# A hybrid layer's kernel: keys laid out by residue, the sample's values in loads of four rows, and an order of five engines computed in the source

## The chip, the core and the metric

One core of a Trainium2 chip runs the whole kernel. The metric is the device time of one execution in microseconds (us). A core has a matrix engine (TensorE; PE in the profile, its weight loads PEld), a vector engine (VectorE, DVE), a scalar engine (ScalarE, ACT), a general engine (GpSimd, POOL) and a sync engine (SyncE, SP). They read and write two on-chip memories, SBUF and PSUM (where matmuls put their sums), of 128 partitions each, and each runs its own list of instructions in order; semaphores hold an instruction back until what it needs is done. All transfers of this kernel (DMAs, transposing ones too) are issued by SP, from one list.

## The reference

One step of a hybrid decoder layer for a prompt of 2048 tokens and a sample of 8 sequences with 8 tokens each. Mixer A is attention over three dilated windows, mixer B a gated linear attention (GLA):

```
h = rmsnorm(x, norm_w);  z = h @ w_in
q, k, v, qb, kb, vb, g_lr, gate_a, gate_b = split(z)
q = rope(rmsnorm(q), pos);  k = rope(rmsnorm(k), pos)        # 8 heads of 64
# for (window, dil) in (128,1), (512,4), (2048,16):
#   softmax over the keys at distance 0, dil, 2*dil, ... window
o_a = sum over the branches of softmax(lse)[branch] * o[branch]
o_b = rmsnorm(gla(qb, kb, vb, log_sigmoid(g_lr @ w_gate_up + b_gate) / 16, s0))
y = x + concat(o_a * silu(gate_a), o_b * silu(gate_b)) @ w_out
```

For the sample the keys and values of the past come from caches of 2048 rows for each sequence (`cache_k_win`, `cache_v_win`). Beside `y` the new keys, values and GLA states are returned.

## The kernel before

The prompt is cut into 16 tiles of 128 tokens. A projection of a tile is a chain of f16 matmuls over 8 blocks of the model's width, in three products of high and low halves (L1120); the normed and rotated queries and keys go to DRAM as f16 (`qp_d`, `kp_d`) and come back transposed by DMA, so that the head's dimension lies along the partitions.

The program is written in the order of its stages. `first(m)` projects v, q and k of the four tiles of block m (m = 0 to 3). For each block and each half of the heads (`pp` = 0, 1) follow the units of attention: `unit(m, pp, 1, x)` is branch 1 (128 consecutive queries against that block of keys and the one before), `unit(m, pp, 2, x)` is branch 2 (the queries of the 512-row block with residue x modulo 4, against the same residue of this block and the one before). `branch3(r)` does residue r modulo 16 over the whole prompt. A unit's pieces go through `attend`: scores on PE (L408), mask and row maximum on DVE (L416), the exponential on ACT (L419), transposes of the probabilities on PE (L426), their copies to SBUF on DVE, ACT or POOL (L389 to L393), the product with v on PE (L441), and the sum of the two halves on DVE (L458).

The block's keys lie in `kk`, a tile [128, 8 heads, 2 slots, 512]: a slot holds one block of 512 keys in their own order, and blocks alternate between the slots. `keys(m, a)` (L841) fills it by a transposing DMA of 128 consecutive rows. `queries(m, pp)` (L853) does the same for the queries, and `swapped` makes on DVE (L845, L846) a second copy of a query tile with the halves of the partitions exchanged. In a score matmul the queries are the stationary operand (PEld) and the keys the moving one. So branch 1 moves runs of consecutive keys, and branch 2 every fourth key, `k[:, :, x::4]`: 256 keys, or 128 in block 0, which has no block before it. Branch 3 loads its own `T_q` and `T_k` (L936, L938) by transposing DMAs of every sixteenth row and swaps the queries with the same two DVE copies.

Woven into these stages are the later projections (qkb, g, vb, gb) and, for the sample's keys, products on POOL with a reduction on DVE (`pr` L980, `sck` L981). Then come the GLA (L120 to L300) and the output stage: the branches are combined, transposed (`tm` L1453, `mt_s` L1465 for the sample) and projected (`Y`, `Y_s` L1488), with the residual added on DVE (L1495). Woven into the output stage is the sample's attention: for each of four pairs of sequences, `sample_pair` loads the cache's values piece by piece (`sv` L1763, 256 KB, one row of the sequence to each partition, eight buffers) and multiplies them on PE with f32 operands (`OS` L1737): 14 steps, one for the new tokens and 13 for pieces of the cache, each step four matmuls that write four column groups of one PSUM tile.

The order is set in three ways: `weave` and the credit of `pump` interleave generators in the source; the tile framework then reorders every engine's list by a simulation of its own; and for a few instructions the source overrules it (`manual_schedule` on ACT around `prep_first`, `issue_after` on two weight loads in `first`).

## Time and profile before

| | us |
|---|---|
| median of 3 runs | 1424.39 |
| lowest and highest run | 1419.62, 1426.09 |
| span of the profiled execution | 1424.9 |
| PE busy in it | 1285.0 |
| DVE busy | 1018.0 |
| ACT busy | 843.7 |
| POOL busy | 621.9 |

The profiled execution's own time is its span, from the first to the last instruction of its one core; what lies around it isn't listed. The page gives each engine's busy time as a share of that span. A view by windows gives the busy time of each engine in a stretch of the span together with the mean clock that the throttle granted to TensorE (PEclk, 1.00 is full speed). The view of waits says what an engine's next instruction waited for, in all, how often, and the longest. A timeline lists runs of the same instruction: start, length, and the count. For `OS` the trace holds two records for each matmul (256 for 128 instructions with `P3x`); all other matmuls quoted here have one.

### The profile page before, as it was taken

Reading aid. Unit: us, or ns where it says so; the run is one execution under the profiler, and the core shown is the slowest. Engines: PE = TensorE matmul, PEld = TensorE weight load, DVE = VectorE, ACT = ScalarE, POOL = GpSimd, SP = SyncE. Lnnn points to the kernel's source line nnn. Section 1 sums busy time; section 2 is a strip of 40 time slices with the busy share of each in tenths; the row PEclk is TensorE's granted clock in tenths of the full one; section 3 lists DMA queues with packets and bytes.
Section 4 is the critical chain, followed back from the end, with each engine's and each line's share of the span. In section 5 each row is a group of like instructions: output and inputs, shape, how many; then the busy total and the mean of one; then the engine's idle time right before and its main releaser. Section 6 shows DMA issues by size and latency. Waiting matters only on the chain.

```text
span 1424.9 us, 26506 instructions
## 1 busy us (share of the span) xinstructions
PE 1285.0 (90%) x8942; PEld 743.6 (52%) x8942; DVE 1018.0 (71%) x2459; ACT 843.7 (59%) x2259; POOL 621.9 (44%) x564
## 2 busy tenths in 40 slices
PE   5989999889898898996889999889999989999997
PEld 2434555455455554664667666666555434444343
DVE  6797697789798967666775357898877797773222
ACT  6466787667377775875677665777876542221120
POOL 0144355566577455554421486556551264340000
PEclk9999999999999899997999999999999999999998
DMA  8469756678966797888976444242235759998661
GB/s 297 156 188 255 192 161 150 182 203 215 240 165 173 208 288 239 260 217 228 234 190 179 149 123 116 87 153 91 88 119 176 267 179 344 359 316 267 221 215 63
DMA packets 246874, 283.27 MB, mean 199 GB/s; under 512 B 117889, under 2 KB 148690, under 8 KB 246738
## 3 DMA queue, kind: packets, MB, share of 16 engines
q1 hardware_dynamic: 246738, 281.57, 67.1%
q8 instruction: 71, 1.16, 0.4%
q14 instruction: 65, 0.53, 0.1%
HBM read 183.19 MB, written 75.24 MB: 181 GB/s over the span
## 4 chain that ended last, share of the span: by engine, by line
PE 35%; DVE 25%; DMA 16%; ACT 11%; issue 7%; POOL 4%; SPq 2%; DVEq 0%; POOLq 0%; ACTq 0%
PE Y L1488 7%; PE acc_g L1120 3%; PE acc_vb L1120 3%; PE acc_k L1120 3%; DMA k<-in_cache_k_win 2%; POOL pr L980 2%; PE s L408 2%; PE OS L1737 2%; PE acc_qkb L1120 2%; ACT p L419 2%; DMA o_d<-o 2%; DMA oc<-o_d 2%; DVE p L416 2%; PE acc_v L1120 2%; DMA T_q<-qp_d 2%
## 5 line engine op out<-in xcount | busy, mean ns | idle before, releaser
L980 POOL TENSOR_TENSOR pr<-k,qb 128x512 f32<-128x512 f32 x128 | 171.8, 1342 | 184.9 <-DVE sck L981 113.9
L1120 PEld LDWEIGHTS <-hr 128*128 128x128 f16 x1824 | 177.7, 100 | 138.2 <-issue 17.6
L419 ACT ACTIVATE p<-p,o 128x256 f32<-128x256 f32 (+1 forms) x384 | 173.1, 453 | 86.0 <-DVE o L416 83.3
L1120 PEld LDWEIGHTS <-hl 128*128 128x128 f16 x1248 | 123.2, 100 | 146.6 <-issue 22.2
L1488 PE MATMUL Y<-w_o,mh 128*128 128x512 f16 x768 | 182.9, 385 | 8.3 <-ACT mh L1454 4.9
L416 DVE CUSTOM_DVE_ANT_0 p<-s,m3w,scl_s 128x256 f32<-128x256 f32 (+1 forms) x384 | 143.6, 419 | 39.0 <-DMA o_d<-o 20.3
L393 POOL TENSOR_TENSOR pt<-p,pt 128x512 f16<-128x512 f32 (+1 forms) x80 | 98.3, 1229 | 139.6 <-ACT pt L392 107.3
L441 PE MATMUL O<-v,pt 128*128 128x128 f16 x1200 | 116.1, 224 | 25.3 <-POOL pt L393 10.0
L426 PE MATMUL t<-ident,p 128*128 128x128 f32 x600 | 119.0, 289 | 14.5 <-ACT p L419 9.2
L1488 PEld LDWEIGHTS <-mh 128*128 128x128 f16 x768 | 72.5, 99 | 103.7 <-issue 25.2
L408 PE MATMUL s<-kk,qq 128*128 128x256 f16 (+1 forms) x512 | 105.7, 326 | 17.5 <-DVE o L416 12.4
L981 DVE TENSOR_REDUCE sck<-pr 128x8 f32<-128x512 f32 x128 | 87.0, 680 | 44.0 <-POOL pr L980 43.7
L441 PEld LDWEIGHTS <-pt 128*128 128x128 f16 x1200 | 86.6, 101 | 54.6 <-POOL pt L393 13.6
L1120 PE MATMUL acc_g<-w_g,hr 128*128 128x272 f16 (+1 forms) x768 | 103.3, 285 | 1.9 <-DVE so_g L677 1.0
L1120 PE MATMUL acc_v<-w_v,hl 128*128 128x512 f16 x384 | 99.5, 405 | 4.6 <-DMA hl<-ht 3.7
L426 PEld LDWEIGHTS t<-ident,p 128*128 128x128 f32 x600 | 73.5, 146 | 43.2 <-ACT p L419 26.4
L1120 PE MATMUL acc_q<-w_q,hl 128*128 128x512 f16 x384 | 92.0, 380 | 1.9 <-ACT zs_q L703 1.4
L1120 PE MATMUL acc_k<-w_k,hl 128*128 128x512 f16 x384 | 91.3, 382 | 2.5 <-ACT w_k L658 1.3
L1454 ACT ACTIVATE mh<-tm 128x1024 f16<-128x1024 f16 x32 | 31.7, 1019 | 104.1 <-PE tm L1453 97.7
L1120 PE MATMUL acc_gb<-w_gb,hr 128*128 128x512 f16 x384 | 90.0, 388 | 2.1 <-DVE so_gb L677 2.1
L1120 PE MATMUL acc_vb<-w_vb,hr 128*128 128x512 f16 x384 | 89.3, 379 | 1.6 <-DVE so_g L677 1.6
L212 ACT ACTIVATE E<-D_e 128x256 f32<-128x256 f32 (+1 forms) x168 | 67.7, 411 | 27.1 <-DVE ks L219 17.6
(533 smaller groups left out, 2628.1 us busy)
## 6 DMA issues: line engine op xcount, KB each, us to landing
k<-in_cache_k_win SPq DMA_DIRECT2D x104, 256.0 KB, 4.3
sv<-in_cache_v_win SPq DMA_DIRECT2D x104, 256.0 KB, 5.4
hr<-h_d SPq DMA_DIRECT2D x44, 512.0 KB, 4.1
qb<-q_d SPq DMA_DIRECT2D x64, 256.0 KB, 4.6
oc<-o_d SPq DMA_DIRECT2D x48, 264.0 KB, 5.8
o_d<-o SPq DMA_DIRECT2D x64, 132.0 KB, 3.9
x<-in_x_prompt SPq DMA_DIRECT2D x16, 512.0 KB, 5.8
h_d<-hl SPq DMA_DIRECT2D x16, 512.0 KB, 4.7
```

The costliest lines, as they stand in the source:

```text
L212: ACT.activation(E[rows, i, :n], D[rows, half], AF.Exp, scale=1.0 / 16.0)
L393: POOL.tensor_tensor(l, f, h, ALU.subtract)
L408: PE.matmul(s_ps[:, i * w : (i + 1) * w], q, k, start=(n == 0), stop=(n == len(prods) - 1),)
L416: DVE.tensor_tensor_reduce(s[:, sl], s_ps[:, sl], mask, neg, BIG, ALU.add, ALU.min, nmf(i))
L419: ACT.activation(s[:, sl], s[:, sl], AF.Exp, bias=nmf(i), scale=-1.0, accum_out=denf(i))
L426: PE.transpose(p_ps[:, i * P : (i + 1) * P], t["s"][:, i * P : (i + 1) * P], ident[:])
L441: PE.matmul(o_, t["pt"][:, c, (i * nb + b) * P : (i * nb + b + 1) * P], vf(i, b), start=(n == 0), stop=(n == 2 * nb - 1),)
L980: POOL.tensor_tensor(pr[:], kt, qt, ALU.mult)
L981: DVE.tensor_reduce(out, pr[:].rearrange("p (u k d) -> p u k d", u=2, k=4), AX.X, ALU.add)
L1120: PE.matmul(z, a_[:, k, :], w[:, p_, k, cols], start=(k == 0 and i == 0), stop=(k == KT - 1 and i == 2),)
L1454: ACT.activation(mhl[:, a], pt[:], AF.Copy)
L1488: PE.matmul(Y[:], a_[:, k, :], w_[:, part, k, :512], start=(i == 0), stop=(i == len(prods) - 1),)
```

## The change

It has three parts.

**Keys by residue.** `kk` becomes [128, 8 heads, 4 residues, 2 slots, 128]. `keys(m, a)` transposes the rows a, a+4, a+8, ... of the 512-row block in place of 128 consecutive rows. Branch 2 then reads its 256 keys (the two slots of one residue) as one consecutive run; branch 1 reads its keys as runs of 32, one for each residue and block of 128. The order of branch 1's keys is thus permuted, and with it the rows of its `v` load and a copy of the mask, `m1w`. The queries stay as they were.

**Values in loads of four rows.** A pair's 26 loads of `sv` become 8: for each of its two sequences one of 256 KB ("w") and three of 1 MB ("b2", "b30", "b34"), each with four neighbouring rows of 2 KB to a partition, in six buffers of 1 MB and two of 256 KB. The weight of the sample's attention in `weave` goes from 64 steps to 36.

**A planner.** At the end of the source `Plan` reads all traced instructions with the tiles they touch, builds their dependencies (`dep`), the order that tiles and buffers force (`behind`), a price for each instruction (`price`), and its longest way to the end of the program (`rank`). `order` is a list scheduler for all five engines at once, which always takes the ready instruction with the longest way to the end, except that on PE it keeps f32 matmuls together (`bias`). `fix` chains each engine's list into a fixed order. `manual_schedule` and `issue_after` are removed. Some constants move between pools, `ident8` is gone.

```
-            r0 = 512 * m + P * a
-            SP.dma_start_transpose(kk[:, :, m % 2, P * a : P * a + P], kp_d[r0 : r0 + P, :])
+            SP.dma_start_transpose(
+                kk[:, :, a, m % 2, :], by4(kp_d[512 * m : 512 * m + 512, :])[a]
+            )
...
-                SP.dma_start(vt[:], sel(vp_d[:, pp * 512 : (pp + 1) * 512]))
+                rows = sel(vp_d[:, pp * 512 : (pp + 1) * 512])
+                SP.dma_start(vt[:], by4(rows) if br == 1 else rows)
...
+                    k = kk[:, 4 * pp + 2 * a + i]
+                    q = [qs_[m, pp][:, order_, 2 * a + i] for order_ in range(2)]
                     if br == 2:
-                        qs = slice(x, 512, 4)
-                        of = lambda k: k[:, :, qs] if nb == 2 else k[:, m % 2, qs]
+                        k = k[:, x] if nb == 2 else k[:, x, m % 2]
+                        q = [f[:, x::4] for f in q]
                     else:
...
+                        k = k.rearrange("p r s (b c) -> p r (s b) c", c=32)
+                        k = k.rearrange("p r b c -> p b r c")[:, of]
...
-        with tc.manual_schedule(engines={mybir.EngineType.Activation}):
-            prep_first(load_w("v"))
+        prep_first(load_w("v"))
...
-                                with tc.issue_after(last_low[0].ins):
-                                    at_once(load_w("q"))
+                                at_once(load_w("q"))
...
+            pieces.append((
+                "b2", [lambda x, c=c: p2[:, x, 32 * c : 32 * c + 32] for c in range(4)],
+                lambda v: v[W - 512 : W, :].rearrange("(j r) c -> j r c", r=4),
+            ))
...
-                    v = ssk.tile([P, 512], F32, name=f"sv_{bp}_{bb}_{i}", tag="sv", bufs=8)
+                    v = ssk.tile(
+                        [P, n, 512], F32, name=f"sv_{bp}_{bb}_{nm_}", tag=f"sv{n}",
+                        bufs=2 if n == 1 else 6,
+                    )
...
-        weave(out, [sample_attention(), 4 * 16])
+        weave(out, [sample_attention(), 4 * 9])
+
+    plan = Plan(tc, nc)
+    far = plan.rank()
+    plan.fix(plan.order([-f for f in far], 2000.0)[1])
```

The parts of the new class that the order rests on:

```
    def price(self):
...
                if ts[0].dtype == F32 and i.is_transpose:
                    busy, late = 109.0 * max(1.0, n / 128), 272.0
                elif ts[0].dtype == F32:
                    busy = max(108.0, 1.69 * n)
                    late = busy + 165
                    self.slow.add(len(self.busy))
                else:
                    n *= 2 if step >= 4 else 1
                    busy, late = max(n / 2.4 + 2.4, 55.5), 165 + n / 2.4
...
            elif e == "SP":
                if kind == "InstDmaTransposeAnt":
                    total = cells(ts[0]) * ts[0].ap[0][1] * 2
                    busy = 1400.0 if total < 500000 else 2800.0
                    late = 18.0 * total / 256 / 16
                    self.lands[len(self.busy)] = 1700.0
...
    def rank(self):
...
            far[n] = max(
                own + max((far[x] for x in self.nxt[n]), default=0.0),
                max((far[x] for x in self.then[n]), default=0.0),
            )
        return far

    def order(self, prio, bias=0.0):
...
            line = now[e]
            if e == "PE" and wide:
                if not line or wide[0][0] <= line[0][0] + (bias if mode else -bias):
                    line = wide
            _, n = heappop(line)
            out[e].append(n)
...
    def fix(self, out):
...
        for e, order in out.items():
            for a, b in zip(order, order[1:]):
                self.tc.add_manual_dep(
                    self.ins[b], self.ins[a].name, info, reason="planned order"
                )
```

The change moves instructions on every engine. Two places follow. The first is PE in the output stage. Before, a stretch with the last `P2x` step and the first matmuls of the first `P3x` step of the first pair (`sv_0_0_5` is pair 0, sequence 0, piece 5; `Y_4` the output projection of tile 4; `mh` its operand):

```order
L1737 MATMUL OS_0_14734<-sv_0_0_4_14817,P2x_14478 32x256
L1488 LDWEIGHTS mh_4_15121
L1488 MATMUL Y_4_1_15279<-w_o1_14251,mh_4_15121 128x512
L1737 MATMUL OS_0_14734<-sv_0_1_4_14819,P2x_14478 32x256
L1737 MATMUL OS_0_14734<-sv_0_0_4_14817,P2x_14478 32x256
L1737 MATMUL OS_0_14734<-sv_0_1_4_14819,P2x_14478 32x256
L1488 LDWEIGHTS mh_4_15121
L1488 MATMUL Y_4_1_15279<-w_o1_14251,mh_4_15121 128x512
L1737 MATMUL OS_0_14734<-sv_0_0_5_14885,P3x_14476 32x256
L1488 LDWEIGHTS mh_4_15121
L1488 MATMUL Y_4_1_15279<-w_o1_14251,mh_4_15121 128x512
L1737 MATMUL OS_0_14734<-sv_0_1_5_14887,P3x_14476 32x256
```

A step's first matmul stands apart from its other three here. Now the same kind of step, of the fourth pair:

```order
L1985 LDWEIGHTS mh_10_15977
L1985 MATMUL Y_10_1_16119<-w_o1_14248,mh_10_15977 128x512
L2234 MATMUL OS_3_16448<-sv_3_0_b2_16461,P2x_14475 32x256
L2234 MATMUL OS_3_16448<-sv_3_1_b2_16463,P2x_14475 32x256
L2234 MATMUL OS_3_16448<-sv_3_0_b2_16461,P2x_14475 32x256
L2234 MATMUL OS_3_16448<-sv_3_1_b2_16463,P2x_14475 32x256
L2234 MATMUL OS_3_16448<-sv_3_0_b2_16461,P2x_14475 32x256
L2234 MATMUL OS_3_16448<-sv_3_1_b2_16463,P2x_14475 32x256
```

Over the whole list the 224 `OS` matmuls stand in 61 runs before (22 of one matmul, 21 of three, 13 of four, 4 of twenty, one of seven), and in 21 runs now (four each of eleven, ten and four, two each of nine and eight, one each of 45, 24, 15, 5 and 1).

The second place is branch 3 on SP and DVE. `T3_q_4` and `T3_k_4` are the transposed loads of residue 4, `k3`, `k2` and `qb` loads for the sample's keys, `o3_d` a store. Before, on SP:

```order
L936 DMA_TRANSPOSE T3_q_4_8281<-qp_d_74 128x8x128
L992 DMA k3_7_0_7905<-in_cache_k_win 128x512
L955 DMA o3_d_69<-o3_0_7822 128x528
L938 DMA_TRANSPOSE T3_k_4_8283<-kp_d_73 128x8x128
L990 DMA qb_7_0_7903<-q_d_58 128x512
```

Now:

```order
L1481 DMA k3_7_5_8224<-in_cache_k_win 128x512
L1425 DMA_TRANSPOSE T3_q_4_8275<-qp_d_74 128x8x128
L1427 DMA_TRANSPOSE T3_k_4_8277<-kp_d_73 128x8x128
L1051 DMA hr_0_8434<-h_d_72 128x2048
L1242 DMA zqk_d_61<-zq_8_8413 128x512
```

The two loads of a residue now follow each other. On DVE, the swapped copies of `T3_q_3` and `T3_q_4` stood eight rows apart, with two sums of `O`, a copy of probabilities and score reductions between them:

```order
L845 COPY T3_q_3_8161<-T3_q_3_8161 64x1024
L846 COPY T3_q_3_8161<-T3_q_3_8161 64x1024
L981 TENSOR_REDUCE sck_6_7179<-pr_3_6_6_7635 128x2x4
L458 TENSOR_TENSOR o3_0_7822<-O3_0_0_8054,ol_260_8066 128x4x64
L981 TENSOR_REDUCE sck_6_7179<-pr_2_6_6_7638 128x2x4
L389 SCALAR_TENSOR_TENSOR pt_3_1_0_8077<-t_3_1_0_8069,pt_3_1_0_8077 128x512
L458 TENSOR_TENSOR o3_0_7822<-O3_0_1_8101,ol_263_8122 128x4x64
L981 TENSOR_REDUCE sck_6_7179<-pr_3_6_3_7727 128x2x4
L845 COPY T3_q_4_8281<-T3_q_4_8281 64x1024
```

Now forty rows lie between them; the last of these:

```order
L902 ISA p_3_3_0_8194,o3_3_8163<-s_3_3_0_8193,m3w_396,scl_s_404 128x128
L902 ISA o3_3_8163 128x1
L1470 TENSOR_REDUCE sck_7_7896<-pr_3_7_1_8110 128x2x4
L1332 COPY T3_q_4_8275<-T3_q_4_8275 64x1024
L1333 COPY T3_q_4_8275<-T3_q_4_8275 64x1024
L902 ISA p_3_3_1_8255,o3_3_8163<-s_3_3_1_8254,m3w_396,scl_s_404 128x128
```

The copies of residue 4 come after the masks of residue 3's first half.

More of the change, by code (lines that the diff above doesn't have):

```diff
@@ L105, in tile_hymba @@
     nw = const("nw", [P, KT], A["norm_w"][0].rearrange("(k p) -> p k", p=P))
-    ident8 = cp.tile([P, P], F32, name="ident8")
-    DVE.tensor_scalar(ident8[:], ident[:], 0.125, None, ALU.mult)
-    ident64 = cp.tile([P, 64], F32, name="ident64")
-    for r0 in (0, 64):
-        DVE.tensor_copy(ident64[r0 : r0 + 64], ident8[r0 : r0 + 64, r0 : r0 + 64])
     ident16 = cp.tile([P, P], F16, name="ident16")
@@ L315, in by16, with by4 @@
         return ap.rearrange("(i r) c -> r i c", r=16)[r]
+    def by4(ap):
+        return ap.rearrange("(c r) f -> r c f", r=4)
     def chain(*gens):
@@ L1020, in tile_hymba @@
         fetch_w("q", places=q_place)
-        with tc.manual_schedule(engines={mybir.EngineType.Activation}):
-            prep_first(load_w("v"))
+        prep_first(load_w("v"))
         fetch_w("k")
         gnw = const1("gnw", [P, P], A["gla_norm_w"].to_broadcast([P, P]))
-        m3w = const1("m3w", [P, 384], A["c_m3"])
+        m3w = const1("m3w", [P, 384], A["c_m3"], pool=ap_)
+        m1w = ap_.tile([P, 384], F32, name="m1w", bufs=1)
+        by_c, by_r = "p (b c r) -> p b r c", "p (b r c) -> p b r c"
+        DVE.tensor_scalar(
+            m1w.rearrange(by_r, r=4, c=32), m3w.rearrange(by_c, r=4, c=32),
+            1e-10, None, ALU.mult,
+        )
         DVE.tensor_scalar(m3w[:], m3w[:], 1e-10, None, ALU.mult)
-        masks12 = (m3w[:, 0:256], m3w[:, 128:384])
+        masks12 = [(w[:, 0:256], w[:, 128:384]) for w in (m1w, m3w)]
         m3 = m3w[:, 128:256]
-        tabs = kp.tile([P, 2, 2, 64], F32, name="tabs")
+        tabs = ap_.tile([P, 2, 2, 64], F32, name="tabs", bufs=1)
         scl = {n_: kp.tile([P, 1], F32, name=f"scl_{n_}") for n_ in "qks"}
@@ L1059, in tile_hymba @@
         DVE.reciprocal(unq[:], scl["q"][:])
-        kk = ap_.tile([P, NH, 2, 512], F16, name="kk", tag="kk", bufs=1)
+        kk = ap_.tile([P, NH, 4, 2, P], F16, name="kk", tag="kk", bufs=1)
         from collections import deque
@@ L1243, in tile_hymba @@
         Sbd = []
-        st = {"wgu": wgu, "E": [], "ks": [], "qbd": []}
+        ident64 = gst.tile([P, 64], F32, name="ident64")
+        for r0 in (0, 64):
+            DVE.tensor_scalar(
+                ident64[r0 : r0 + 64], ident[r0 : r0 + 64, r0 : r0 + 64], 0.125, None, ALU.mult
+            )
+        st = {"wgu": wgu, "ident64": ident64, "E": [], "ks": [], "qbd": []}
         for i in range(2):
```

483 lines of the change are left out of this document (449 added, 34 removed).

## The prediction

> **What bounds the kernel now.** I read the page first, then busy time by stretches of the span, then the waits and the timeline at the places that the change touches. From the page:
>
> ```profile
> span 1424.9 us, 26506 instructions
> PE 1285.0 (90%) x8942; PEld 743.6 (52%) x8942; DVE 1018.0 (71%) x2459; ACT 843.7 (59%) x2259; POOL 621.9 (44%) x564
> PE 35%; DVE 25%; DMA 16%; ACT 11%; issue 7%; POOL 4%; SPq 2%; DVEq 0%; POOLq 0%; ACTq 0%
> ```
>
> PE is busy for nine tenths of the span, so time can go in two ways: PE's own work gets shorter, or its 140 us of idle time (1424.9 − 1285.0) go. The chain that ended last lies on PE for a third only; in the attention stages it hops between DVE, ACT and DMA, so PE's idle time is made by hand-overs between engines, which an order can change. Where the idle time lies shows the view by windows (columns: the stretch, its length, then busy time and instruction count of PE, PEld, DVE, ACT and POOL, then PEclk, the DMA share and GB/s):
>
> ```profile
> 0.00:40.00 40.00, 22.83 (x137) 12.55 (x138) 29.13 (x79) 24.15 (x40) 0.85 (x7) 1.00 0.86 299
> 40.00:250.00 210.00, 195.50 (x1139) 105.17 (x1138) 166.71 (x408) 139.12 (x379) 86.51 (x76) 0.98 0.66 180
> 250.00:360.00 110.00, 99.35 (x647) 57.97 (x646) 93.81 (x209) 75.99 (x205) 67.42 (x51) 0.98 0.75 206
> 360.00:500.00 140.00, 121.57 (x787) 73.03 (x786) 121.03 (x260) 93.08 (x257) 86.46 (x64) 0.93 0.75 194
> 500.00:880.00 380.00, 348.68 (x2624) 229.20 (x2622) 242.87 (x740) 255.92 (x798) 187.93 (x172) 0.96 0.75 204
> 880.00:1000.00 120.00, 107.05 (x1011) 77.32 (x1010) 104.39 (x220) 95.05 (x250) 68.10 (x84) 0.97 0.35 112
> 1000.00:1200.00 200.00, 180.06 (x1213) 97.33 (x1210) 160.47 (x346) 119.96 (x273) 84.33 (x84) 0.97 0.58 190
> 1200.00:1400.00 200.00, 192.90 (x1333) 83.72 (x1326) 93.96 (x200) 40.08 (x61) 40.25 (x31) 0.99 0.79 268
> 1400.00:1425.00 25.00, 17.07 (x68) 7.29 (x68) 5.66 (x8) 0.38 (x1) 0.00 (x0) 0.82 0.13 43
> ```
>
> Length minus PE busy gives 17.2 us in the first 40, 107.8 us from 40 to 1200 (14.5, 10.7, 18.4, 31.3, 13.0, 19.9), 7.1 us in the output stage and 7.9 us in the tail. In three stretches DVE is within a sixth of the length too (93.81 of 110, 121.03 of 140, 104.39 of 120): there PE's idle time, 42.1 us together, can't go without DVE becoming the bound. The other 65.7 us have no second engine above 81%.
>
> **The keys.** In a score matmul only the moving operand's layout changes. The same matmul, 256 keys, stands in the trace in both layouts; the first two rows are scores by length and start, all of branch 1 in one stretch and all of branch 2 in another, the rest timeline rows:
>
> ```profile
> L408 PE MATMUL s<-kk,qq x16: 269/272/273, 299.9 to 308.5; 128*128 128x256 f16 x16
> L408 PE MATMUL s<-kk,qq x32: 389/409/414, 599.9 to 624.9; 128*128 128x256 f16 x32
> 308.19 0.60 PE L408 MATMUL s<-kk,qq 128*128 128x256 f16 x4
> 308.63 1.67 PE L1120 MATMUL acc_v<-w_v,hl 128*128 128x512 f16 x7
> 605.22 1.08 PE L408 MATMUL s<-kk,qq 128*128 128x256 f16 x4
> 606.12 1.04 PE L1120 MATMUL acc_qkb<-w_qkb,hr 128*128 128x512 f16 x4
> L408 PE MATMUL s<-kk,qq 128*128 128x256 f16 x432 | 93.8, 335 | 17.5 <-DVE o L416 12.4 <-DMA kk<-kp_d 5.0
> L408 PE MATMUL s<-kk,qq 128*128 128x128 f16 x80 | 11.9, 277 | 0.0
> ```
>
> Four matmuls hold PE for 0.44 us (308.19 to 308.63) with consecutive keys and for 0.90 us (605.22 to 606.12) with every fourth key: 0.11 and 0.23 each, a difference of 0.12, which the median lengths confirm (409 − 272 = 137 ns). Branch 2 has 256 score matmuls, 64 of them on block 0 with 128 keys; 192 × 0.12 + 64 × 0.06 = 27 us of PE. Branch 1 now reads runs of 32 keys. No row has such runs; at one extra step per run it costs nothing one can see, and at the price of the strided read 240 × 0.12 + 16 × 0.06 = 30 us come back. Within a run the elements touch, so I take 0. Bounds of the term: 27 gained to 3 lost. Some of the 27 falls into the stretch 360 to 500, where DVE has 121 of 140 us and would wait for its masks no less; I take two thirds, **−18 us**. The transposing loads with strided source rows, and the permuted v loads, have a neighbour in branch 3, which reads every sixteenth row (`T_q`):
>
> ```profile
> kk<-kp_d SPq DMA_TRANSPOSE x16, 4.8
> T_q<-qp_d SPq DMA_TRANSPOSE x16, 4.1
> ```
>
> It lands no later (4.1 against 4.8 us), so strided source rows cost 0; the loads hide behind the blocks' other projections, and if that cover went, PE would wait some 4 us for each of four blocks.
>
> [...]
>
> **The values.** The bytes are the same (104 × 256 KB before; 8 × 256 KB and 24 × 1 MB now), the issues on SP fall by 72. What they cost now is on PE, in the output stage, where f32 `OS` matmuls stand between f16 ones (two records per `OS` matmul):
>
> ```profile
> 1327.73 1.48 PE L1737 MATMUL OS<-sv,P2x 128*32 128x256 f32 x24
> 1329.14 0.44 PE L1663 MATMUL R<-ident,Scg 128*128 128x128 f32 x2
> 1337.12 0.63 PE L1737 MATMUL OS<-sv,P3x 128*32 128x256 f32 x6
> 1337.69 0.82 PE L1488 MATMUL Y<-w_o,mh 128*128 128x512 f16 x3
> 1338.44 0.62 PE L1737 MATMUL OS<-sv,P3x 128*32 128x256 f32 x2
> 1338.99 1.04 PE L1488 MATMUL Y<-w_o,mh 128*128 128x512 f16 x4
> 1339.96 0.64 PE L1737 MATMUL OS<-sv,P3x 128*32 128x256 f32 x8
> 1340.53 0.39 PE L1488 MATMUL Y<-w_o,mh 128*128 128x512 f16 x1
> ```
>
> A run of twelve matmuls, three steps, takes 1.41 us until the next work; a run of four 0.57, of three 0.57, of one 0.55. So a step costs (1.41 − 0.57) / 2 = 0.42, and a run 0.15 beside it; a lone matmul costs as much as four, since a step's matmuls fill four column groups side by side. The f16 work after a run loses some more: four `Y` take 0.97 (1338.99 to 1339.96) where four take 0.88 in the tail (10.52 / 48 each, by the last row of the next section), 0.1 us per run. Before, by the counts of the order: 22 lone matmuls at 0.65, 34 runs of three or four at 0.67, four of twenty at 0.25 + 5 × 0.42 = 2.35, one of seven at about 1.1: 47.6 us. Now 56 steps at 0.42, 21 runs at 0.25 and some 12 steps that are still cut at about 0.3: 32.4 us. That is **−15 us**. The bounds are 0 (PE has only 7.1 us of idle time there, so nothing hides it) to −19, if no step were cut. SP's wait for buffers of `sv` is long,
>
> ```profile
> SPq L1763 <- PE OS L1737: 47.7, 23, 8.2
> ```
>
> and behind it stand the loads of the next tiles; with six buffers of 1 MB, SP still waits for a buffer, and I take no gain from it.
>
> **The tail.** The last rows of PE's timeline:
>
> ```profile
> 1394.78 3.63 PE L1488 MATMUL Y_s<-w_o,mh_s 128*128 128x512 f16 x16
> 1402.51 0.69 PE L1465 MATMUL mt_s<-ident,mix_s 64*128 64x64 f32 x4 [4.11 <-DVE mix_s L1566]
> 1404.13 6.03 PE L1488 MATMUL Y_s<-w_o,mh_s 128*128 128x512 f16 x16 [0.94 <-DVE mh_s L1471]
> 1410.00 10.52 PE L1488 MATMUL Y<-w_o,mh 128*128 128x512 f16 x48
> ```
>
> PE waits 5.05 us for the sample's last output, and the 16 `Y_s` after it take 6.03 in place of 3.63: 7.4 us. In the new order more than a whole `Y` tile (over 10 us by the last row) stands between the last `OS` and `mt_s`, so the way through DVE and two DMAs is covered. **−6 us**, bounds 0 and −7.4.
>
> **The order of the attention and GLA stages.** This is the largest term and the least certain. Of the 107.8 us of idle time I take half of the 65.7 us that lie where no second engine is near its end, 33, and a sixth of the 42.1 where DVE is, 7: **−40 us**. Nearly nothing is certain in it. The upper bound is all 107.8 gone. The lower bound is a loss, worked out under the rivals: a fixed list can wait where the old one did. The first 40 us I leave as they are: they wait for inputs (DMA share 0.86).
>
> Sum: 1424.9 − 18 − 15 − 6 − 40 = 1345.9, **1346 us**. The sum is made against the span of one execution, 1424.9, which is 0.5 us above the median of three.
>
> **Rivals.**
>
> *One DVE instruction behind a late load (slower).* In branch 3 DVE's list holds the two copies of the swapped queries, and whatever stands behind them waits for the transposed load. It happened before:
>
> ```profile
> DVE T_q L845 <- DMA T_q<-qp_d: 9.6, 4, 5.2
> PE t L426 <- ACT p L419: 6.5, 2, 5.3
> 647.53 6.97 DMA T_q<-qp_d
> 655.00:685.00 30.00, 19.42 (x132) 14.52 (x133) 25.01 (x86) 21.95 (x77) 11.88 (x9) 0.66 0.79 213
> ```
>
> The load took 6.97 us, DVE waited up to 5.2 us for it, the masks behind it were late, PE waited 5.3 us for ACT's exponential, and in the 30 us after that the granted clock was 0.66: 10.6 us idle and 19.42 × 0.34 = 6.6 us of slow clock, 17 us for one event. The planner gives a transposing load one landing time; the new list moves the copies, with a residue's two loads next to each other on SP. If its landing times are too short, a residue's copies stop DVE. There are 16 residues, the query loads of branches 1 and 2, and stores and reloads by DMA in the GLA stage. The gains above come to 79 us, so from 79 / 17 = 4.6 such events the change decides for slower. At six it is 1346 + 102 = **1448 us**. Against it: in the order shown a residue's copies have moved behind forty rows of other work, which gives the load more time than the eight rows before. Chance 0.17.
>
> [...]
>
> *The plan buys nothing in the attention (DVE binds).* There DVE is busy for up to 0.87 of a stretch, with masks and sums that hand work to ACT and back; if hand-overs and not order make the idle time, and much of the keys' gain turns into waiting for DVE, there remain −15, −6 and −4: **1400 us**. For it speaks that the old list came from a simulation as well. Chance 0.13.
>
> *The stride isn't the cost, or the runs of 32 cost as much.* Then −18 becomes 0: **1364 us**. The rows above speak against the first, none against the second. Chance 0.08.
>
> *The idle time nearly goes.* With 85 of 107.8 us gone and the clock up with it, 1425 − 18 − 15 − 6 − 85 = **1301 us**. It needs prices that are right within some 0.1 us on five engines. Chance 0.11.
>
> *Late loads and gains cancel.* Four or five events of the first kind: **1424 us**, chance 0.05.
>
> **How the numbers follow.** The forecast keeps 0.46; with its own bounds on keys and order it lies between 1320 and 1375. The case of 1301 and most of the case of 1400 belong into a range of 8 in 10, and it must reach to where the slower case begins: 1290 to 1430, which leaves out most of the slower case and a little below. A measurement of this kernel tells 0.5% (7 us; the three runs lie 6.5 apart) from no change. Faster by more than that: 0.46 + 0.13 + 0.08 + 0.11 = 0.78; within it 0.05; slower 0.17.
>
> **What would show it.** Keys: all score matmuls of 256 keys near 272 ns, branch 1's too; branch 1 above 350 would show the runs' cost. Values: lengths of `OS` unchanged, with some 20 runs in place of 61, and PE busy in the output stage down by about 15 us. Tail: no wait of `mt_s` above 1 us and a clock near 1.00 in the last 25 us. Order: PE idle between 40 us and the output stage near 68 us in place of 108, and PEclk nowhere under 0.9. The forecast is wrong if DVE's waits for `T_q` or `qq` loads grow beyond 30 us, or if the granted clock falls in several stretches; then PE's busy time grows though its work shrank.

## The result, and the profile after

| | median us | runs | lowest and highest |
|---|---|---|---|
| before | 1425.24 | 4 | 1419.62, 1427.01 |
| changed | 1388.16 | 4 | 1386.43, 1392.19 |

The ratio is 0.9746, with a 95% interval of 0.9721 to 0.9770: 36 us faster, where 79 were forecast. The profiled execution of the changed kernel has a span of 1385.1 us. From its page:

```profile
span 1385.1 us, 26375 instructions
PE 1244.2 (90%) x8942; PEld 739.4 (53%) x8942; DVE 1008.1 (73%) x2459; ACT 844.7 (61%) x2259; POOL 639.5 (46%) x564
```

PE's busy time fell by 40.8 us (1285.0 to 1244.2). Its idle time did not fall at all: 139.9 us before, 140.9 now. So in sum the whole gain is work that PE no longer does. (What the new order buys by itself, and what the layouts cost in idle time, is taken apart in e3 and e4 below.) Where the idle time lies shows the view by windows, cut at the same points of the program in both kernels: the last score with keys of `kk`, the last product of the attention, the first `tm` of the output stage, and the end. Before:

```profile
0.00:624.90 624.90, 557.08 (x3513) 320.90 (x3514) 494.01 (x1175) 421.49 (x1132) 312.93 (x253) 0.97 0.75 210
624.90:803.20 178.30, 155.35 (x1291) 111.10 (x1290) 117.50 (x433) 127.37 (x441) 59.86 (x54) 0.93 0.77 197
803.20:1142.30 339.10, 313.00 (x2439) 196.00 (x2437) 256.33 (x543) 233.96 (x593) 181.18 (x205) 0.98 0.45 139
1142.30:1424.90 282.60, 259.56 (x1705) 115.57 (x1703) 150.19 (x310) 60.93 (x95) 67.88 (x54) 0.97 0.73 246
```

The changed kernel:

```profile
0.00:585.90 585.90, 509.34 (x3410) 306.78 (x3411) 485.34 (x1171) 414.84 (x1112) 325.15 (x258) 0.98 0.80 221
585.90:755.90 170.00, 157.16 (x1308) 106.91 (x1307) 111.38 (x425) 129.49 (x447) 50.17 (x42) 0.98 0.80 211
755.90:1135.90 380.00, 338.93 (x2528) 209.28 (x2526) 275.56 (x575) 243.69 (x614) 202.15 (x218) 0.94 0.43 131
1135.90:1385.10 249.20, 238.79 (x1702) 116.40 (x1702) 135.86 (x290) 56.73 (x88) 62.01 (x47) 0.99 0.73 273
```

(Columns as in the prediction: length, then PE, PEld, DVE, ACT, POOL.) The attention ends 47 us earlier and the output stage is 33 us shorter, but the stage between, the GLA with the way into the output stage, is 41 us longer: PE's busy time in it grew by 26 us, and its idle time grew from 26.1 to 41.1 us. One wait of 19.26 us is more than that growth, a row of PE's timeline with its cause in brackets:

```profile
1135.85 0.82 PE L1950 MATMUL tm<-ident,mt 128*128 128x128 f16 x6 [19.26 <-ACT mt L1940]
```

The parts that the prediction priced look as follows after the change: scores of branch 2 (560 to 586 us) and branch 1 (290 to 310 us), `OS` runs, and the tail.

```profile
L894 PE MATMUL s<-kk,qq x40: 272/273/273, 561.4 to 585.9; 128*128 128x256 f16 x40
L894 PE MATMUL s<-kk,qq x24: 269/273/417, 291.4 to 309.6; 128*128 128x256 f16 x24
...
1187.87 1.93 PE L2234 MATMUL OS<-sv_b,P3x 128*32 128x256 f32 x30
1189.73 2.55 PE L1985 MATMUL Y<-w_o,mh 128*128 128x512 f16 x11
...
1361.80 7.08 PE L1985 MATMUL Y_s<-w_o,mh_s 128*128 128x512 f16 x32 [0.97 <-DVE mh_s L1968]
1369.64 10.59 PE L1985 MATMUL Y<-w_o,mh 128*128 128x512 f16 x48 [0.76 <-DVE xr_s L1992]
```

Both branches' scores take 273 ns at the median, where branch 1's took 272 and branch 2's 409 before; the runs of 32 keys cost nothing that these lengths show. Fifteen `OS` matmuls in one run take 1.86 us to the next work, 0.12 each, as the twelve in 1.41 us did before. In the tail the waits are 0.97 and 0.76 us, and the 32 `Y_s` take 0.22 us each, as the `Y` behind them.

### The profile page after: what moved, and what is told of

Same layout as the page of the kernel before. It is cut to its first block, busy times and chain, and to the rows that moved or that the text cites. A ratio compares the mean times of both kernels' runs of the same rounds, so it can differ in the third digit from the quotient of the medians.

```text
span 1385.1 us, 26375 instructions
## 1 busy us (share of the span) xinstructions
PE 1244.2 (90%) x8942; PEld 739.4 (53%) x8942; DVE 1008.1 (73%) x2459; ACT 844.7 (61%) x2259; POOL 639.5 (46%) x564
## 4 chain that ended last, share of the span: by engine, by line
PE 36%; DVE 8%; ACT 7%; DMA 6%; issue 3%; POOL 1%; SPq 1%; DVEq 0%; ACTq 0%; POOLq 0%
PE Y L1985 10%; PE acc_vb L1614 4%; PE acc_g L1614 4%; PE acc_gb L1614 4%; DMA qb<-q_d 2%; PE OS L2234 1%; PE sc_e L730 1%; ACT p L905 1%; PE t L912 1%; PE O L1791 1%; PE acc_qkb L1614 1%; DMA o_d<-o 1%; DVE qbd L706 1%; PE O L1785 1%; PE O L927 1%
## 5 line engine op out<-in xcount | busy, mean ns | idle before, releaser
L927 PE MATMUL O<-v,pt 128*128 128x128 f16 x1200 | 145.9, 224 | 8.6 <-POOL pt L879 3.5
L1614 PE MATMUL acc_g<-w_g,hr 128*128 128x272 f16 (+1 forms) x768 | 130.6, 276 | 3.3 <-ACT vbs L1263 2.0
L1614 PE MATMUL acc_vb<-w_vb,hr 128*128 128x512 f16 x384 | 122.1, 384 | 1.6 <-DVE so_g L1163 1.5
L1614 PE MATMUL acc_v<-w_v,hl 128*128 128x512 f16 x384 | 120.2, 384 | 2.0 <-DMA hl<-ht 1.0
L1614 PE MATMUL acc_k<-w_k,hl 128*128 128x512 f16 x384 | 114.8, 379 | 4.5 <-DVE vp L1276 2.9
L1614 PE MATMUL acc_q<-w_q,hl 128*128 128x512 f16 x384 | 116.2, 379 | 2.8 <-ACT zs_q L1189 2.4
L894 PE MATMUL s<-kk,qq 128*128 128x256 f16 (+1 forms) x512 | 84.8, 270 | 29.4 <-DVE o L902 21.7
L902 DVE CUSTOM_DVE_ANT_0 p<-s,m3w,scl_s 128x128 f32<-128x128 f32 (+1 forms) x256 | 87.8, 396 | 19.8 <-DMA o_d<-o 8.9
L2033 POOL TENSOR_TENSOR tc<-oc,w 128x512 f32<-128x512 f32 x32 | 42.8, 1354 | 118.7 <-DVE w L2025 67.9
L1614 PE MATMUL acc_qkb<-w_qkb,hr 128*128 128x512 f16 x288 | 85.1, 379 | 0.0
```

What stands on the lines that cost most here:

```text
L894: PE.matmul(s_ps[:, i * w : (i + 1) * w], q, k, start=(n == 0), stop=(n == len(prods) - 1),)
L902: DVE.tensor_tensor_reduce(s[:, sl], s_ps[:, sl], mask, neg, BIG, ALU.add, ALU.min, nmf(i))
L927: PE.matmul(o_, t["pt"][:, c, (i * nb + b) * P : (i * nb + b + 1) * P], vf(i, b), start=(n == 0), stop=(n == 2 * nb - 1),)
L1614: PE.matmul(z, a_[:, k, :], w[:, p_, k, cols], start=(k == 0 and i == 0), stop=(k == KT - 1 and i == 2),)
L2033: eng.tensor_tensor(t_[:], oc[:, g, :, 0:64], w[:, g].unsqueeze(2).to_broadcast([P, NH, HD]), ALU.mult,)
```

## The experiments

All are run beside the kernel before on the same chip; the ratio to it is what is compared. Differences between two runs are differences of these ratios times 1425 us, and are uncertain by some 5 to 9 us. "Keys", "values" and "plan" are the three parts of the change.

| run | what it holds | median us | ratio to before, interval |
|---|---|---|---|
| e1 | keys | 1444.27 | 1.0146 (1.0103 to 1.0189) |
| e2 | values | 1414.25 | 0.9925 (0.9900 to 0.9951) |
| e3 | plan | 1407.98 | 0.9893 (0.9844 to 0.9943) |
| e4 | keys, values | 1433.83 | 1.0066 (1.0042 to 1.0090) |
| e5 | keys, block 0 in pieces | 1438.35 | 1.0099 (1.0062 to 1.0136) |
| e6 | plan, values | 1398.82 | 0.9807 (0.9767 to 0.9846) |
| e7 | plan, keys | 1394.86 | 0.9783 (0.9744 to 0.9823) |
| the change | plan, keys, values | 1388.16 | 0.9746 (0.9721 to 0.9770) |
| e8 | the change, gb held back | 1377.03 | 0.9651 (0.9612 to 0.9690) |
| e9 | the change, thin reductions | 1373.01 | 0.9621 (0.9586 to 0.9655) |
| e10 | plan, values, thin reductions | 1382.88 | 0.9697 (0.9658 to 0.9735) |
| e11 | e8, one copy on ACT | 1374.55 | 0.9615 (0.9580 to 0.9651) |
| e12 | e8, margin 200 ns | 1350.29 | 0.9483 (0.9456 to 0.9509) |
| e13 | e8, margin 0 | 1394.52 | 0.9795 (0.9762 to 0.9828) |
| e14 | e8, prices of reads | 1369.71 | 0.9621 (0.9594 to 0.9648) |
| e15 | e12 without keys | 1346.27 | 0.9480 (0.9443 to 0.9518) |
| e16 | the change, margin 200 ns | 1351.49 | 0.9515 (0.9488 to 0.9543) |
| e17 | e8, margin 400 ns | 1381.06 | 0.9712 (0.9676 to 0.9748) |
| e18 | e12 and e14 together | 1357.07 | 0.9556 (0.9523 to 0.9588) |

### The three parts, alone and in pairs (e1 to e4, e6, e7)

The kernels without the planner are the changed one with its last three lines out and the two overrides of the framework's order back; the ones without a layout part have the old lines of it.

```
-    plan = Plan(tc, nc)
-    far = plan.rank()
-    plan.fix(plan.order([-f for f in far], 2000.0)[1])
...
+        with tc.manual_schedule(engines={mybir.EngineType.Activation}):
+            prep_first(load_w("v"))
```

> Keys by residue alone, in the framework's own order (values and planner as before). Theory 1, that the two layout parts shorten PE's work by their full price and the planned order is worth nothing net: 1398 to 1407 us, with scores of branch 2 near 272 ns and PE busy down by 25 to 28 us. Theory 2, that the layouts' gain is swallowed by DVE unless the planner reorders: 1413 to 1425 us, PE busy down but PE idle up by as much.

Slower by 1.5%, outside both ranges. The page of this run, and the score matmuls of it and of the kernel before:

```profile
PE 1266.5 (88%) x8942; PEld 739.7 (51%) x8942; DVE 1025.2 (71%) x2459; ACT 844.9 (59%) x2259; POOL 622.9 (43%) x564
...
L894 PE MATMUL s<-kk,qq x512: 216/272/421, 141.8 to 644.1; 128*128 128x256 f16 x144, 128*128 128x128 f16 x27
```

```profile
L408 PE MATMUL s<-kk,qq x512: 216/280/421, 113.0 to 624.9; 128*128 128x256 f16 x144, 128*128 128x128 f16 x27
```

PE's work fell by 18.5 us and its idle time rose by 36.6 (1443.0 − 1266.5 against 139.9). The first score starts 28.8 us later, because one residue of a block has rows of all four tiles: where a unit of branch 1 needed its own tile's keys (and the one before), it now needs the k projection of the whole block. Nothing in the source says so; it follows from which rows a load reads.

> Values in loads of four rows alone, in the framework's own order: its OS matmuls stand in 9 runs in place of 61. Theory 1: 56 steps at 0.42 and 9 runs at 0.25 make 26 us in place of 47.6, so 1403 to 1408 us. Theory 2, that PE waits for the 1 MB pieces without the planner: 1415 to 1430 us, with waits of OS for its loads above 10 us.

Between the two: 10.7 us faster by the ratio (0.0075 × 1425). PE's busy time fell by 23.5 us (to 1261.5, of a span of 1414.3), more than the price by runs and steps gave (47.6 − 26 = 22), but idle time rose by 13. The waits of PE show new ones in the output stage, for other things than the loads:

```profile
PE Y L1980 <- DVE xr L1987: 10.8, 3, 4.6
...
PE T L2208 <- ACT spr L2195: 7.4, 2, 5.6
```

> The planner alone, keys and values as before (OS in 46 runs). Theory 1: within 0.5% of before, 1418 to 1432 us, PE idle near 140 us. Theory 2, that the order is worth something by itself: 1395 to 1412 us with PE idle below 125 us.

Theory 2: the planner alone is worth 15 us (0.0107 × 1425), with 124.0 us of PE idle (span 1404.4, busy 1280.4). Where that idle time lies, cut at the same points of the program:

```profile
0.00:590.70 590.70, 532.41 (x3410) 312.58 (x3411) 487.94 (x1173) 413.67 (x1111) 329.23 (x262) 0.98 0.81 222
590.70:763.50 172.80, 158.20 (x1307) 107.54 (x1306) 108.94 (x421) 130.11 (x447) 45.77 (x39) 0.97 0.78 198
763.50:1145.90 382.40, 340.53 (x2535) 210.55 (x2534) 276.78 (x578) 244.14 (x615) 203.93 (x218) 0.94 0.42 130
1145.90:1404.40 258.50, 249.23 (x1695) 116.27 (x1693) 140.44 (x287) 56.68 (x87) 62.42 (x47) 0.98 0.78 264
```

Against the kernel before, PE's idle time fell by 18 us in the two stretches of the attention (58.3 and 14.6 us, from 67.8 and 23.0) and by 14 in the output stage (9.3 from 23.0), and it rose by 16 in the stage between (41.9 from 26.1), where PE now waits once for a load of the sample:

```profile
1142.66 0.69 PE L2126 MATMUL ts_q<-ident,ls_q 64*128 64x64 f32 x4 [18.21 <-DMA ls_q<-q_d]
```

From 40 us (15.9 us of idle time lie before that, 17.2 in the old kernel) to the first `tm` it is 98.9 us, where it was 99.7: over the stretch that the prediction's term for the order is about, the order alone removed nothing in sum.

> Both layout parts without the planner, in the framework's own order. Theory 1: as fast as the whole change, 1378 to 1390 us, PE idle near 140 us. Theory 2: 1398 to 1412 us, the rest of the gain being the planner's.

Slower than before, and outside both ranges. So theory 1 falls: the two layout parts don't add up to the change without the planner. From its page:

```profile
span 1432.9 us, 26392 instructions
PE 1249.9 (87%) x8942; PEld 744.1 (52%) x8942; DVE 1022.5 (71%) x2459; ACT 844.0 (59%) x2259; POOL 623.9 (44%) x564
```

PE's work fell by 35 us and its idle time rose by 43, to 183.0 us. On top of the two layouts the planner is then worth 46 us (1.0066 − 0.9746), three times what it is worth alone, and brings the idle time back to 140.9. So the three parts don't add, and how much of the 36 us belongs to which of them depends on the order in which they are added.

> The whole change without the keys by residue (keys in their own order; planner and values as changed). Theory 1, that the keys are worth some 10 us under the planner, since they start the attention 45 us later (162.7 against 117.6 us): 1395 to 1402 us. Theory 2, that they are worth their full 27 us of PE: 1410 to 1417 us. Theory 3, nothing: 1386 to 1391 us.

> The whole change without the larger loads of values (OS in 46 runs in place of 21). Theory 1, the price by run and step (41 against 32 us of PE): 1394 to 1400 us. Theory 2, that the planner hides the loads' split: 1386 to 1391 us.

Both came out as theory 1 said. With the planner the keys are worth 9 us (0.9807 − 0.9746, e6 against the change) to 16 (e3 against e7), the values 5 (e7) to 12 (e3 against e6), each give or take 7 to 9 by the intervals, so that the 5 is not clear of nothing. The planner is what turns the keys from a loss of 21 us into a gain. A part of that is the time up to the first score, now at 162.7 us: the planner fills it with projections, so that PE is idle for 5.5 us only between 40 us and there (12.0 in e1). The larger part lies behind: from the first to the last key score PE is idle for 55.2 us in the change and for 67.2 in e1.

### Is it the wait for the block's keys? (e5)

```
+            if m == 0:
+                rows = kp_d[P * a : P * a + P, :]
+                for r in range(4):
+                    SP.dma_start_transpose(kk[:, :, r, 0, 32 * a : 32 * a + 32], by4(rows)[r])
+            else:
```

> Keys by residue alone as in the first experiment (1444 us), but block 0's keys come in pieces of 32 rows, one for each tile and residue, so that the first unit needs only the first tile's keys again. Theory 1, that the layout's price is the wait for all four tiles of a block, which starts the attention 29 us later: first score near 113 to 122 us in place of 142, and 1412 to 1428 us. Theory 2, that the framework orders the attention worse for another reason: first score earlier, but 1436 us or more.

```profile
L894 PE MATMUL s<-kk,qq x512: 216/272/421, 119.9 to 631.4; 128*128 128x256 f16 x144, 128*128 128x128 f16 x27
```

The first score came back to 119.9 us, as theory 1 said, but the time is theory 2's: the ratio moved from 1.0146 to 1.0099 only. From first to last key score it is 511.5 us here and 511.9 before, though PE is busy for 436.8 us of it here and for 469.4 before. So the wait before the first block explains a part (the last score ends 13 us sooner than in e1). The larger part stays: in the old order the length of this stage doesn't follow PE's work. What it follows is not shown; blocks 1 to 3 still wait for four tiles here (PE waits for `kk` five times, 12.5 us in all, against 5.0 before), and that was not tried apart.

### The passage into the output stage (e8)

The row with 19.26 us of idle time has a simple ground. First and last start of the gb projections and of the last matmuls of the GLA, before and then after:

```profile
L1120 PE MATMUL acc_gb<-w_gb,hr x384: 376/379/634, 1009.0 to 1142.1; 128*128 128x512 f16 x192
L1294 PE MATMUL O<-vb,full x128: 272/275/377, 884.4 to 1108.3; 128*128 128x128 f32 x128
```

```profile
L1614 PE MATMUL acc_gb<-w_gb,hr x384: 377/379/635, 939.0 to 1113.2; 128*128 128x512 f16 x192
L1791 PE MATMUL O<-vb,full x128: 272/275/422, 861.9 to 1103.2; 128*128 128x128 f32 x128
```

From the GLA's last matmul to the first `tm` (1142.3 and 1135.9 us) it is 34 us before and 33 after: stores, loads, the combination on DVE and POOL. Before, gb projections ran up to the end of it; the planner, which always takes what is ready, had used them inside the GLA and had 10 us of them left. The experiment holds four tiles back:

```
+    touched = [[t for t, _, _ in acc] for acc in plan.acc]
+    pe = [n for n in range(plan.real) if plan.eng[n] == "PE"]
+    last = max(n for n in pe if any(t.startswith("O_15_") for t in touched[n]) and any("vb_15" in t for t in touched[n]))
+    for n in pe:
+        if any(t.startswith(("acc_gb_12", "acc_gb_13", "acc_gb_14", "acc_gb_15")) for t in touched[n]):
+            plan.dep[n].add(last)
```

> The whole change, with the gb projections of the last four tiles (20.7 us of PE) held back behind the last matmul of the GLA. Theory 1, that the planner spent the work which covered the passage from the GLA to the output stage: the wait of tm for ACT falls from 19.3 us to under 10, and 1374 to 1383 us. Theory 2, that the GLA stage then idles for as long as the gap shrinks: 1385 to 1391 us.

Theory 1: 13.5 us by the ratio. In the stage between, idle time falls from 41.1 to 27.3 us (it rises by 5 in the output stage), and the wait is nearly gone:

```profile
PE tm L1950 <- ACT mt L1940: 2.5, 1, 2.5
```

### Does DVE swallow the keys' gain? (e9 to e11)

```
-                out, pr[:].rearrange("p (u k d) -> p u k d", u=2, k=4), AX.X, ALU.add
+                out, pr[:, 0:64].rearrange("p (u k d) -> p u k d", u=2, k=4), AX.X, ALU.add
```

> The whole change, but the 128 reductions of the sample's key products on DVE read 64 of their 512 elements, so that about 61 us of DVE's work between 204 and 680 us are left out (the sample's scores are not the reference's). Theory 1, that DVE bounds the stretch of 250 to 500 us and swallows the keys' gain: 1388 falls to 1350 to 1368 us. Theory 2, that hand-overs and the fixed order bound it: 1376 to 1388 us.

> The same work left out, with the keys in their old layout (1398.8 us with full reductions). Theory 1: with DVE relieved PE bounds, and the keys' layout is worth its whole 25 to 27 us of PE, so this is 20 to 27 us above the run before it. Theory 2: it stays at some 11 us above.

e9 falls between its two ranges, e10 where theory 2 put it. DVE's busy time is 52.8 us shorter in e9 than in the change (1008.1 to 955.3) and 54.1 shorter in e10 than in e6 (1008.8 to 954.7). This gave 18 and 16 us, about a third of it, and the keys' worth with it is 11 us (0.9697 − 0.9621), give or take 7, where it was 9 without. So at this planner's prices DVE's load is a cost like others, and taking this much of it away does not give the keys their 20 to 27 us. That DVE still binds in part is not excluded: between the first and the last key score it is busy for 77% of e9, against 85% in the change.

```
-            DVE.tensor_copy(q[64:128, 1], q[0:64, 0])
+            ACT.activation(q[64:128, 1], q[0:64, 0], AF.Copy)
```

> The version with the gb projections of four tiles held back (1377 us), and one of the two swapped copies of each query tile moved from DVE to ACT (some 12 us off DVE, some 30 us onto ACT). Theory 1: 1368 to 1375 us. Theory 2: 1375 to 1382 us.

Inconclusive: its interval and that of e8 overlap. DVE's busy time fell by 13.7 us (1017.2 in e8 to 1003.5) and ACT's rose by 28.4 (844.9 to 873.3).

### Hand-overs in fixed lists (e12 to e18)

A stretch of the changed kernel's timeline on DVE, POOL and PE shows how idle time can arise:

```profile
304.49 1.20 DVE L614 SCALAR_TENSOR_TENSOR qr_qk<-ra_qk,rr_qk 128x16 f32<-128x16 f32 x1
305.69 0.69 DVE L1470 TENSOR_REDUCE sck<-pr 128x8 f32<-128x512 f32 x1
306.30 1.22 DVE L1225 TENSOR_TENSOR t_qk<-t_qk,qr_qk 128x1024 f32<-128x1024 f32 x1
307.43 0.48 DVE L902 CUSTOM_DVE_ANT_0 p<-s,m1w,scl_s 128x256 f32<-128x256 f32 x1
```

```profile
304.38 1.28 POOL L1469 TENSOR_TENSOR pr<-k,qb 128x512 f32<-128x512 f32 x1
```

```profile
305.22 0.38 PE L1614 MATMUL acc_k<-w_k,hl 128*128 128x512 f16 x1
308.37 0.60 PE L894 MATMUL s<-kk,qq 128*128 128x256 f16 x4 [2.78 <-DVE o L902]
```

The mask (L902) stands behind a DVE instruction of 128x16 elements that took 1.20 us (0.175 is the median of its twelve), to 305.69 us, where POOL's product ended at 305.66, and behind two more; the next scores on PE wait 2.78 us for the mask, and nothing behind them in PE's list may go ahead. The planner prices a hand-over between engines at 35 ns; the experiments change that price (and, in e14, two others that the trace corrects).

```
-    def __init__(self, tc, nc, cross=35.0, traffic=1.15, lanes=8, room=212832):
+    def __init__(self, tc, nc, cross=200.0, traffic=1.15, lanes=8, room=212832):
```

> The version with gb held back (1377 us), with the planner's price of a hand-over between engines raised from 35 to 200 ns, so that a consumer is placed later behind its producer on every engine. Theory 1, that the attention's idle time comes from hand-overs that arrive a little later than planned, in lists that can't step past them: idle time of PE before the last key score falls below 70 us (78 in that version), 1360 to 1372 us. Theory 2, that the wider margin only lengthens every chain: 1378 to 1395 us.

> The same version with the hand-over's price at 0 ns. Theory 1: consumers placed closer, 1380 to 1395 us with more idle time before the last key score. Theory 2: 1370 to 1378 us.

> The same version with two prices corrected by the trace: the mask on DVE is done 83 ns later (its accumulator read), the exponential on ACT 110 ns later (its accumulator read of 190 in place of 85). Theory 1, that these mispriced hand-overs of the attention make PE wait: 1362 to 1373 us. Theory 2, that single prices don't matter: 1374 to 1380 us.

The times are on theory 1's side: 24 us faster with 200 ns (0.9651 to 0.9483; more than its range), 20 slower with 0. But its claim on the place fails. Up to the last key score, at 573.0 us, the idle time is 73 us (573.00 − 499.87), not below 70, against 78 in e8; the rest came in the GLA and output stages (376.6 to 365.2 and 254.4 to 246.6 us; idle time there fell by 12 and 6 us) and out of PE's busy time, which fell by 15.5 us in all (1247.8 to 1232.3) with the same number of matmuls, for no cause that these runs show. So what the price of 200 ns is worth is measured; that it works through hand-overs which now come in time is argued, not shown. e12 and then e15:

```profile
0.00:573.00 573.00, 499.87 (x3374) 303.69 (x3375) 486.47 (x1164) 409.53 (x1105) 319.63 (x251) 0.97 0.79 219
735.50:1100.70 365.20, 349.88 (x2660) 217.23 (x2658) 265.51 (x562) 245.07 (x624) 196.28 (x215) 0.99 0.44 138
1100.70:1347.30 246.60, 237.09 (x1702) 116.92 (x1702) 153.13 (x314) 63.73 (x99) 72.10 (x49) 0.98 0.76 282
```

```profile
0.00:573.70 573.70, 513.81 (x3371) 306.71 (x3372) 481.65 (x1167) 410.42 (x1103) 320.16 (x256) 0.98 0.80 222
```

(The two rows of e8 that this compares with:)

```profile
747.00:1123.60 376.60, 349.35 (x2578) 215.84 (x2576) 273.24 (x555) 241.26 (x613) 202.49 (x216) 0.96 0.43 133
1123.60:1378.00 254.40, 238.90 (x1702) 116.54 (x1702) 147.58 (x314) 62.72 (x97) 64.45 (x49) 0.98 0.74 271
```

> Margin of 200 ns and gb held back, but the keys in their old layout (1350.3 us with keys by residue). Theory 1, that late hand-overs swallowed the keys' gain: with the margin the keys are worth 20 to 27 us, so 1370 to 1377 us. Theory 2, that the wait for all four tiles of a block and the attention's own chains swallow it: 10 us as before, 1358 to 1363 us.

Both theories miss: with the margin the keys are worth nothing. The rows above show it: with and without them the last key score falls at 573 us, with 14 us less of PE's work and 13 more of idle time. DVE is busy for 84 to 85% of that stretch in both; whether it sets the floor there was not tried (thin reductions with the margin would tell).

> The whole change as it is, with the margin of 200 ns alone (gb not held back). If margin and held gb add up: 1359 to 1364 us, with the wait of tm for ACT still near 19 us. If the margin mends the passage by itself: 1348 to 1354 us.

> Gb held back and a margin of 400 ns. Theory 1 (hand-overs late by some tenths of a us): little more to gain, 1345 to 1355 us. Rival, that the margin lengthens the chains beyond their real length: 1358 us or more.

> Gb held back, the margin of 200 ns and the corrected prices of the accumulator reads. If the two mend the same lateness: 1347 to 1353 us. If they add up: 1340 to 1346 us.

The margin alone gives 33 of the 37 us (0.9746 to 0.9515) that margin and held gb give together. By the ratio that is 1356 us, between the two forecasts: the causes overlap, and PE still waits 13.9 us once in the passage, for a load of the sample (`ls_q`). 400 ns is too much, the rival of e17. And e18 should have been as fast as e12 or faster; it is 10 us slower (0.9556 to 0.9483). Every edit of a price makes a new plan on all five engines, and such plans can differ by some 10 us, as these two do, for no cause that these runs show. So e8's 13 us rest on the wait that vanished, and the margin's 24 to 33 us are beyond that, but e14's 4 us and e11's 5 are not results. The same caution holds for the 5 to 16 us of keys and values under the planner, which compare two plans each.

e12 and e15 are the fastest versions found: 5.2% below the kernel before, and 2.7% below the change.

## Why the prediction was right or wrong

**Right:** the direction, the place of each price on PE, and the tail. PE's busy time fell by 40.8 us, where the two layouts' prices come to 27 + 15 = 42. Score matmuls of 256 keys take 273 ns in both branches, in branch 2 in place of 409. The tail is 5.9 us shorter where 6 were forecast (3.63 + 6.03 + 5.05 before, 7.08 + 0.97 + 0.76 now). The waits of DVE for `T_q`, the mechanism of the slower rival, fell to 3.5 us from 20.5, so that rival was wrong:

```profile
DVE T_q L845 <- DMA T_q<-qp_d: 20.5, 10, 5.2
DVE T_q L1332 <- DMA T_q<-qp_d: 3.5, 3, 1.7
```

**Wrong in the term of the order, −40 us.** The step was "half of the 65.7 us that lie where no second engine is near its end, 33, and a sixth of the 42.1". It treated idle time as if an order could remove it where it lies. The prediction's own sign was near 68 us of idle time between 40 us and the output stage in place of 108; cut at the first `tm`, it was 99.7 us before, and is 98.9 with the planner alone (e3) and 114.6 in the change. What the runs show is that it moves: in e3 the attention lost 18 us of it, but the gb projections were spent in the GLA, and the passage to the output stage, 33 us long, lost its cover, and the stage that ends with it took 16 back. The 15 us that the planner alone measures lie in the output stage with its tail (14 us of idle time, where 6 were forecast for the tail). Against the 31 us that were missing (46 forecast for order and tail, 15 measured), holding gb back returned 13 in the changed kernel, a price of 200 ns for a hand-over 33, and both together 37.

The sum also added terms that depend on each other. The two layouts without the planner cost 43 us of idle time (e4), of which the sum had 9, the third of the 27; on top of them the planner is worth 46 us, the very size forecast for order and tail. That is luck: the forecast took it from the idle time of the kernel before, and these 46 us only repair what the layouts had cost. Nor does the reason for taking only a sixth of the 42.1 us follow from the rows: in each of the three stretches PE is busier than DVE (99.35 against 93.81, 121.57 against 121.03, 107.05 against 104.39), so DVE would not have become the bound.

**Wrong in a step on the keys, not in their price.** "If that cover went, PE would wait some 4 us for each of four blocks" priced the transfer and not what it waits for: a block's residue needs four tiles' projections. Alone this starts the attention 29 us later. The size was off as well: −18 became −9 to −16 under the planner as it is, 0 with a better order, +21 in the old one. "Two thirds" was taken from DVE's share of a stretch; in e9 and e10 53 and 54 us less on DVE raised the keys' worth by 2 us, within the intervals.

**The values, −15 us,** were right in PE's work when alone (23.5 us, 22 by the price) and too large in time, 11 us, because the output stage then waited for DVE and ACT. "Nothing hides it" was the step: PE was near full there only as long as its own work was that long. Under the planner, 5 to 12 us, the term counted something twice: the planner alone joins the 61 runs of `OS` into 46, so that the loads had only the step from 46 to 21 left, 9 us by the price (41 against 32).

**The rival that DVE binds (1400 us)** came nearest in time. Its mechanism is half borne out: PE's work does not set the attention's length (e5 against before: 511.5 and 511.9 us with 33 us less of PE's busy time; e12 against e15: 573 us in both with 14 less), but that hand-overs with DVE do is not shown, and 53 us off DVE gave about a third of it.

**Open:** what holds the attention at 573 us in the best order, by what way the price of a hand-over saves its 33 us, and what makes plans differ by 10 us.

## What to carry to other kernels

When a part takes work from the busiest engine, ask of the stage whether its length follows that engine: a stage that something else paces gives idle time in exchange for the work removed (here 13 us for 14, e12 against e15). Ask of every relaid load which rows, and so which producers, it now waits for. Parts of a change need not add: the planner is worth 15 us alone and 46 on top of the layouts, so a sum of terms that were each priced on the old kernel has to say what each leaves for the next. And work that fills gaps is also the cover of the next passage: a scheduler that always takes what is ready spends it early. Its price for a hand-over is worth trying out: 0, 35, 200 and 400 ns gave ratios of 0.980, 0.965, 0.948 and 0.971.

## What the runs showed of the hardware

One instruction of DVE with one element to a partition (three in one of its 14 runs) took 0.16 us at the median and 1.68 us at one place, in the changed kernel; there it ended at 312.32 us, and POOL's product that ran beside it at 312.30. The first row gives its shortest, median and longest length in ns.

```profile
L614 DVE SCALAR_TENSOR_TENSOR rs<-ra_x,rr_x x14: 144/159/1680, 9.8 to 364.3; 128x1 f32<-128x1 f32 x13, 128x3 f32<-128x3 f32 x1
310.64 1.68 DVE L614 SCALAR_TENSOR_TENSOR rs<-ra_x,rr_x 128x1 f32<-128x1 f32 x1
```

```profile
309.95 2.35 POOL L1213 TENSOR_TENSOR t_qk<-zs_q,ct_qk 128x1024 f32<-128x1024 f32 x1
```

POOL had started at 309.95, DVE at 310.64, and the two ended within 0.02 us of each other; what held DVE's instruction until then is not shown.

Also new was the price of reading an accumulator, which follows each mask on DVE (83 ns at the mean, 384 times) and each exponential on ACT (190 ns, 384 times):

```profile
L902 DVE DVE_READ_ACCUMULATOR2_ANT o<- 128x1 f32 x384 | 31.7, 83 | 0.1
```

```profile
L905 ACT ACTIVATION_READ_ACCUMULATOR p<-p,o 128x1 f32 x384 | 73.1, 190 | 0.0
```

The median score matmul of branch 3 (128 keys) took 311 ns from 655 to 685 us of the kernel before, where the granted clock was 0.66, and 219 ns from 690 to 760 us, at 0.98.
